# Retention and attention query/key projections as seven block products instead of eight, in a two-layer decoder trunk on one Trainium2 core

## The chip, the cores and the metric

The kernel runs on one core of a Trainium2 chip. The core has a matrix engine (PE, TensorE, whose weight loads are listed apart as PEld), a vector engine (DVE), a scalar engine (ACT), a general engine (POOL, GpSimd), a queue engine (SP) that mostly issues DMAs, and 16 DMA engines behind the queues. Matrix results land in PSUM, which this kernel uses as eight banks of 128 x 512 float32. The metric is the device time of one execution in microseconds, the median over runs; lower is better.

## The reference, cut to what matters

Two layers, each of a mixing sublayer and a SwiGLU feed-forward sublayer, on 512 tokens of width 1024, all in float32. The mixing sublayer starts from one wide projection of x, whose columns hold the queries, keys and values of the attention (three head groups of six heads of 64), the queries and keys (four heads of 256) and values and gates (four heads of 512) of the retention, and two merge gates.

```
z = einsum('bsd,dc->bsc', x, w_in) + b_in
q_a, k_a, v_a, q_r, k_r, v_r, g_r, gate_a, gate_b = split(z)
for group in 3 groups:                     # windows (128,1), (512,4), (2048,16)
    s = q k^T * 64**-0.5 + bias(relative position), masked to the window
    o, lse = softmax(s) v, log of the denominator
y_a = sum over groups of softmax(lse) * o

def rot(t):                                # halves t1, t2 of a retention head
    return concat(t1 * cos - t2 * sin, t1 * sin + t2 * cos)
q_r, k_r = rot(q_r), rot(k_r) / 16
y_r = retention(q_r, k_r, v_r)             # scores times a decay, then group norm
merged = sigmoid(gate_a) * (y_a @ w_attn_proj) + sigmoid(gate_b) * (silu(g_r) * y_r) @ w_ret_proj
x = layer_norm(ALPHA * x + merged @ w_out)
x = layer_norm(ALPHA * x + (silu(x @ w_gate) * (x @ w_up)) @ w_down)
```

## The kernel before

**Float32 from three products.** TensorE multiplies operands split in a high part (`act.copy`, a cast) and a low part (`dve.tensor_tensor`, the difference); `hilo` makes both. `mm3` then issues three matmuls: high by high, high by low, low by high. Every weight unit (`raw`, 128 x 1024 = 512 KB, loaded on SP's queue) is turned by `unit` or `Right.high` into `whi` (ACT) and `wlo` (DVE). The input is held transposed as `xh`/`xl`.

**Plain projections.** `pair_units` loads two units that hold 256 columns (two tiles of 128) of the weight over all eight blocks of the depth. `wstat(us, q)` multiplies one tile of 128 columns with all 512 tokens into one PSUM bank: 8 blocks x 3 matmuls of 512 columns. `wstat_halves` does the same in halves of 256 tokens at the kernel's start, for the first head pair, groups 0 and 1.

**Block products.** Most other projections go through `Right`: the product is cut in 2 x 2 blocks and computed with seven block products instead of eight. `ORDER` lists them; `S1` to `S4` are sums of quarters of x (in `xs`, made once per sublayer by `x_sums`), `P1` to `P4` are sums of quarters of the weight. P1 and P3 come from a second load that POOL issues with an addition (`accum_op`), P2 and P4 from an addition on DVE. `wide` runs it with the weights stationary and 256 tokens moving, so each matmul has 256 columns; `CHAIN` keeps three PSUM banks A, X and C, into which several products add up. `Right.operands` prepares the weights of the next product (load, cast on ACT; the low part on DVE is issued when its turn comes) while the current one runs. Before the change `wide` is used in the feed-forward sublayer and the merge gates, `tall` (tokens stationary) in values and gates.

**What runs beside the products.** `side` is a list of small pieces of work. Every step of a product calls `tick`, which takes the next pieces off that list at a rate set by `pace(us)`; `drain` issues all that is left at once. So the order of the instructions on each engine is fixed by hand, by the counts of steps. In the attention, `scores` (matmuls, a minimum on DVE at L536, an exponential on ACT at L538), `turn` (transposes L546, copy L547) and `values` of head pair `hp` are such pieces, and they run beside the projections `qk_units`/`wstat` of head pair `hp + 1`; each of them keeps two PSUM banks from its scores to its values. Two DMA round trips (`exd`, `mb`, `fa`, L574 to L593) that combine the head groups are issued from ACT. In the retention, the scores and outputs of head `h - 1` run beside the rotary, values and gates of head `h`.

**What the change touches.** `rotary(h)`: per query and key two `wstat`; the evacuation multiplies by cosine and sine with the bias added (L668), combines (L672, L673) and splits with `hilo` into a slot named `rot`, a slot per half of the head. `qk_units`, `qk_put` (a `tensor_scalar` on DVE that adds the bias and scales) and the loop over head pairs. `load`, `Right.load`, `bias_cols`, the order of the first loads in `layer`, and `ret_scores`, which reads the `rot` slots.

Of the kernel before, what the change touches and what calls it, by code (L numbers as in the profile page):

```python
# [53 lines left out]
def hybrid_kernel(ctx, tc, x, rel_bias, w_in, b_in, w_attn_proj, w_ret_proj, w_out,  # L54
# [44 lines left out]
    def work(name):  # L99
        return wk.tile([P, S], F32, tag="w2", name=name)  # L100
# [205 lines left out]
    class Right:  # L306
# [7 lines left out]
        def load(self, *names):  # L314
            for n in names:
                if (n, 0) in self.t:
                    continue
                for u, (a, b) in enumerate(self.shapes):
                    r = self.t[n, u] = load(self.src({"P1": "B11", "P3": "B12"}.get(n, n), u), a, b)
                    if n in ("P1", "P3"):  # L320
                        pool.dma_start(r, self.src({"P1": "B12", "P3": "B22"}[n], u), accum_op=ALU.add)  # L321

        def high(self, n):

# [298 lines left out]

    VB = 288

    bTs, braws = [], []
    for ly in range(DEPTH):
        bTs.append(sm.tile([P, COLS // P], F32, tag="bT", name="bT", bufs=2))
        braws.append(work("braw")[:COLS // P, :P])

    def bias_cols(ly):
        n = COLS // P
        px = psum()
        pe.transpose(px[:, :n], braws[ly], ident[:n, :n])
        dve.tensor_copy(bTs[ly], px[:, :n])

    def layer(ly, cp):
        w_l = rows(w_in[ly])
# [15 lines left out]
        def slot(name="op", dt=F32R):  # L654
            return opp.tile([P, 2, S], dt, tag="op", name=name)

        def rotary(h):

            rot = []
            for c0 in (C_QR + h * RQ, C_KR + h * RQ):  # L660
                us = pair_units(w_l, c0)
                prod = []
                for t in range(2):
                    ps = wstat(us, t)
                    pr = []
                    for tb in (cos, sin):
                        m = work("rp")
                        dve.scalar_tensor_tensor(out=m, in0=ps, scalar=bcol(c0 + t * P), in1=tb, op0=ALU.add, op1=ALU.mult)  # L668
                        pr.append(m)
                    prod.append(pr)  # L670
                (t1c, t1s), (t2c, t2s) = prod
                dve.tensor_tensor(out=t1c, in0=t1c, in1=t2s, op=ALU.subtract)  # L672
                dve.tensor_tensor(out=t1s, in0=t1s, in1=t2c, op=ALU.add)  # L673
                pair = []
                for src in (t1c, t1s):
                    o_ = slot("rot")
                    hilo(src, o_[:, 0], o_[:, 1])
                    pair.append(o_)
                rot.append(pair)
            heads[h]["q"], heads[h]["k"] = rot  # L680

        def ret_values_gates(h):
            cv, cg = C_VR + h * RV, C_GR + h * RV
# [18 lines left out]
        with stage("attn") as ap_, stage("attw", 4) as aw:  # L702
# [9 lines left out]
            def qk_put(hp, g, j, ps):  # L712
# [4 lines left out]
                    i_ = i_.rearrange("p (l r) -> p r l", r=4)  # L717
                dve.tensor_scalar(o_, i_, bcol(cc), (HD ** -0.5, 1.0)[j], op0=ALU.add, op1=ALU.mult)

            if ly == 0:  # L720
                x0 = [slot("x0", F32) for _ in range(NI)]
                warm = work("warm")
# [17 lines left out]
                load_x(2)  # L740
# [6 lines left out]
                for f in late:  # L747
                    f()
                us0 = [first, qk_units(0, 1)]
                load_x(3)  # L750
                side.extend([lambda l_=l_: bias_cols(l_) for l_ in range(DEPTH)] + vecs[:3] + ops[2] + vecs[3:] + ops[3])
                dve.tensor_tensor(out=pick, in0=ident[:, :NR], in1=ident[:, BK:BK + NR], op=ALU.add)
                rate[0], credit[0] = 0.4, 0.0
            else:
                us0 = [qk_units(0, g) for g in range(2)]
            for g in range(NG):
                qk_slot(0, g)
            pool.dma_start(cos, c_cos)
            pool.dma_start(sin, c_sin)
# [75 lines left out]
        with stage("ret") as rp:  # L835
            def ret_scores(h):
# [5 lines left out]
                def one(j):  # L842
                    n = S - j * P
                    ps = psum()[:, :n]
                    for d in range(2):
                        k_, q_ = heads[h]["k"][d], heads[h]["q"][d]
                        mm3(ps, k_[:, 0, j * P:(j + 1) * P], k_[:, 1, j * P:(j + 1) * P],
                            q_[:, 0, j * P:], q_[:, 1, j * P:], d == 0, d == 1)
                    t = work("pt")
                    dve.tensor_tensor(out=t[:, :n], in0=ps, in1=dec[:, :n], op=ALU.mult)  # L850
                    sl = heads[h]["p"][j]
# [354 lines left out]
```

## Time and profile before

| | us |
|---|---|
| median of three runs | 2185.17 (2185.1 to 2186.9) |
| the profiled execution | 2185.52 |
| its span in the trace | 2183.7 |
| mean granted TensorE clock | 0.997 |

The profiled execution's time lies 1.8 us above its span, which begins with the first and ends with the last instruction of the trace, and 0.35 us above the median. In the rows, a line such as `149.84 0.40 PE L82 MATMUL ps<-xh,whi` gives the start from the span's beginning, the duration, the engine, the line of the kernel, the operation and its output and inputs; what stands in brackets is the idle time before it and what ended that. Matmuls overlap their neighbours, so the distance between two starts is what one costs, not its duration. The stages of layer 0 in the trace: start to 20 us, first projections and attention values to 100, attention head pairs beside projections 100 to 206, the last pair beside rotary 0 and head 0's values and gates to 294, retention heads 1, 2 and 3 from 294 to 514 in three stretches of 73 us, then output and feed-forward; layer 1 repeats them from 1080 us.

### The profile page before, as it was taken

Reading aid. Unit: us, or ns where it says so; the run is one execution under the profiler, and the core shown is the slowest. Engines: PE = TensorE matmul, PEld = TensorE weight load, DVE = VectorE, ACT = ScalarE, POOL = GpSimd, SP = SyncE. Lnnn points to the kernel's source line nnn. Section 1 sums busy time; section 2 is a strip of 40 time slices with the busy share of each in tenths; the row PEclk is TensorE's granted clock in tenths of the full one; section 3 lists DMA queues with packets and bytes.
Section 4 is the critical chain, followed back from the end, with each engine's and each line's share of the span. In section 5 each row is a group of like instructions: output and inputs, shape, how many; then the busy total and the mean of one; then the engine's idle time right before and its main releaser. Section 6 shows DMA issues by size and latency. Waiting matters only on the chain.

```text
span 2183.7 us, 32442 instructions
## 1 busy us (share of the span) xinstructions
PE 2161.5 (99%) x12906; PEld 1902.4 (87%) x12906; DVE 1396.0 (64%) x2011; ACT 980.6 (45%) x1585; POOL 228.3 (10%) x253
## 2 busy tenths in 40 slices
PE   8999999999999999999999999999999999999998
PEld 7977788889988899989898778888899889999996
DVE  5643677777755685747675346767877447766575
ACT  4444544546633263525245445444556233544350
POOL 4100011011000100010020000111010001000001
PEclk9999999999999999999999999999999999999999
DMA  8944266458685356656269343565577762666551
GB/s 230 235 134 104 59 164 164 135 131 194 190 305 192 88 154 132 171 133 158 93 163 255 89 92 92 140 178 148 137 188 227 260 193 58 175 151 161 125 161 39
DMA packets 304954, 338.60 MB, mean 155 GB/s; under 512 B 21790, under 2 KB 243138, under 8 KB 304673
## 3 DMA queue, kind: packets, MB, share of 16 engines
q1 hardware_dynamic: 227712, 248.81, 37.8%
q0 software_dynamic: 49808, 74.90, 18.1%
q10 hardware_dynamic: 27280, 12.80, 2.1%
q8 instruction: 101, 1.65, 0.3%
q14 instruction: 53, 0.43, 0.1%
HBM read 310.67 MB, written 28.53 MB: 155 GB/s over the span
## 4 chain that ended last, share of the span: by engine, by line
PE 90%; issue 4%; DMA 3%; DVE 2%; POOL 1%; ACT 0%; SPq 0%; POOLq 0%; DVEq 0%; ACTq 0%
PE ps L82 81%; PE px L82 7%; DMA raw<-in_w_in 2%; PE px L546 1%; DMA exd<-wb 1%; PE px L878 1%; POOL ry L125 0%; DMA mb<-exd 0%; DMA exd<-pk 0%; PE px L170 0%; DVE xtok L1001 0%; DVE wlo L336 0%; ACT whi L330 0%; PE px L602 0%; DVE xtok L1010 0%
## 5 line engine op out<-in xcount | busy, mean ns | idle before, releaser
L336 DVE TENSOR_TENSOR wlo<-raw,whi 128x1024 fp32r<-128x1024 f32 (+1 forms) x364 | 417.9, 1150 | 214.1 <-ACT whi L330 212.9
L82 PE MATMUL ps<-xh,whi 128*128 128x256 f32 (+1 forms) x1536 | 516.6, 338 | 4.5 <-ACT whi L93 3.5
L330 ACT CAST whi<-raw 128x1024 fp32r<-128x1024 f32 (+1 forms) x364 | 359.0, 990 | 345.4 <-PE ps L82 205.3
L82 PE MATMUL ps<-xh,wlo 128*128 128x256 f32 (+1 forms) x1536 | 500.9, 327 | 1.0 <-DVE wlo L94 1.0
L82 PE MATMUL ps<-xl,whi 128*128 128x256 f32 (+1 forms) x1536 | 501.2, 327 | 0.2 <-DVE xl L94 0.2
L82 PE MATMUL ps<-xs,whi 128*128 128x256 f32 (+1 forms) x2048 | 404.6, 296 | 0.0
L82 PEld LDWEIGHTS ps<-xs,whi 128*128 128x128 f32 x2048 | 327.7, 191 | 10.3
L94 DVE TENSOR_TENSOR wlo<-raw,whi 128x1024 fp32r<-128x1024 f32 (+2 forms) x162 | 193.3, 1196 | 202.0 <-ACT whi L93 201.0
L82 PEld LDWEIGHTS ps<-xh,whi 128*128 128x128 f32 x1536 | 292.4, 191 | 34.3 <-issue 5.7
L82 PEld LDWEIGHTS ps<-xh,wlo 128*128 128x128 f32 x1536 | 292.9, 191 | 26.5 <-DVE wlo L94 1.2
L82 PEld LDWEIGHTS ps<-xl,whi 128*128 128x128 f32 x1536 | 293.7, 191 | 19.5 <-DVE xl L94 1.0
L82 PE MATMUL ps<-xs,wlo 128*128 128x256 f32 (+1 forms) x1024 | 303.4, 296 | 0.0
L93 ACT CAST whi<-raw 128x1024 fp32r<-128x1024 f32 (+2 forms) x162 | 166.0, 1027 | 240.8 <-PE ps L82 150.7
L82 PE MATMUL ps<-whi,xs 128*128 128x512 f32 (+1 forms) x768 | 219.6, 360 | 0.6 <-ACT whi L330 0.4
L82 PEld LDWEIGHTS ps<-xs,wlo 128*128 128x128 f32 x1024 | 196.0, 191 | 5.0
L82 PE MATMUL ps<-whi,ht 128*128 128x512 f32 x576 | 178.4, 389 | 0.0
L82 PEld LDWEIGHTS ps<-whi,xs 128*128 128x128 f32 x768 | 137.7, 188 | 21.1 <-ACT sn L466 1.0
L82 PE MATMUL ps<-wlo,xs 128*128 128x512 f32 (+1 forms) x384 | 138.1, 360 | 0.8 <-DVE wlo L336 0.8
L321 POOL DMA_DIRECT2D raw<-in_w_in x64 | 79.2, 1263 | 472.9 <-DMA raw<-in_w_in 159.8
L82 PEld LDWEIGHTS ps<-whi,ht 128*128 128x128 f32 x576 | 108.2, 188 | 22.3
L321 POOL DMA_DIRECT2D raw<-in_w_ffn_gate x40 | 51.8, 1295 | 679.4 <-DMA raw<-in_w_ffn_up 251.4
L347 DVE TENSOR_TENSOR raw<-raw 128x1024 f32<-128x1024 f32 (+1 forms) x104 | 119.5, 1149 | 2.7 <-DMA raw<-in_w_in 0.5
(183 smaller groups left out, 2897.0 us busy)
## 6 DMA issues: line engine op xcount, KB each, us to landing
raw<-in_w_in SPq DMA_DIRECT2D x152, 512.0 KB, 4.3
raw<-in_w_ffn_up SPq DMA_DIRECT2D x64, 512.0 KB, 4.1
raw<-in_w_in POOLq DMA_DIRECT2D x48, 512.0 KB, 6.9
raw<-in_w_ffn_gate SPq DMA_DIRECT2D x44, 512.0 KB, 4.6
raw<-in_w_ffn_down SPq DMA_DIRECT2D x44, 512.0 KB, 4.2
raw<-in_w_ffn_gate POOLq DMA_DIRECT2D x40, 512.0 KB, 6.7
raw<-in_w_in SPq DMA_DIRECT2D x72, 256.0 KB, 4.9
raw<-in_w_ret_proj SPq DMA_DIRECT2D x32, 512.0 KB, 6.1
```

Of the source, the lines that this page charges most:

```text
L82: pe.matmul(ps, lhsT=a, rhs=b, start=start, stop=stop, skip_group_check=True)
L93: act.copy(out=hi, in_=src)
L94: dve.tensor_tensor(out=lo, in0=src, in1=hi.bitcast(F32), op=ALU.subtract)
L321: pool.dma_start(r, self.src({"P1": "B12", "P3": "B22"}[n], u), accum_op=ALU.add)
L330: act.copy(out=h, in_=src)
L336: dve.tensor_tensor(out=l, in0=src, in1=h.bitcast(F32), op=ALU.subtract)
L347: dve.tensor_tensor(out=r, in0=r, in1=self.t["B22" if n == "P2" else "B21", u], op=ALU.add)
L546: pe.transpose(px[:, (2 + j) * P:(3 + j) * P], s[:, hh, j * P:(j + 1) * P], ident)
L878: pe.transpose(px[:, t * P:(t + 1) * P], ys[i][:, t * P:(t + 1) * P], ident)
```

## The change

1. `rotary(h)` for heads 1 to 3 computes queries and keys of a head in one `wide` call of seven products (query columns as the left, key columns as the right half of the weight). Head 0 keeps `wstat`. The evacuation works on quarters (two tiles by 256 tokens): the bias is added by ACT (`biased_copy`), quarters are combined on DVE, and `turned` rotates each. The `rot` slots now hold both halves of the head in high and in low part; `ret_scores` reads them so.
2. In the attention's head pairs 1 and 2, groups 0 and 1 go through one `wide` call (`qk_group`): queries of the two groups as the left, keys as the right half. ACT writes the results with bias and scale (`put`; scaled biases of the queries in the new `bQs`). Group 2 keeps `wstat`. A load whose columns lie in two places is issued in two pieces (`pieces`).
3. In layer 0 the cosine and sine tables are loaded on SP's queue behind the four loads of x instead of on POOL's; the third load of x stands later in the program's text.

```diff
     def load(src, a, b):
         v = view(raw(), a, b)
-        nc.sync.dma_start(v, src)
+        for v_, s_ in pieces(v, src):
+            nc.sync.dma_start(v_, s_)
         return v
...
+        act.mul(out=bQs[ly], in_=px[:, C_QA // P:C_QA // P + NQ], mul=HD ** -0.5)
...
+        def turned(t, ts_, hi, lo):
+            n = t.shape[2]
+            s = view(work("rs"), 2, n)
+            cs, sn_ = (a[:, ts_].unsqueeze(1).to_broadcast([P, 2, n]) for a in (cos, sin))
+            dve.tensor_tensor(out=s, in0=t, in1=sn_, op=ALU.mult)
+            dve.tensor_tensor(out=t, in0=t, in1=cs, op=ALU.mult)
+            dve.tensor_tensor(out=t[:, 0], in0=t[:, 0], in1=s[:, 1], op=ALU.subtract)
+            dve.tensor_tensor(out=t[:, 1], in0=t[:, 1], in1=s[:, 0], op=ALU.add)
+            hilo(t, hi[:, :, ts_], lo[:, :, ts_])
         def rotary(h):
...
+            def biased_copy(ps, c, sign=1.0):
+                o_ = view(work("sn"), 2, 256)
+                for q in range(2):
+                    act.activation(out=o_[:, q], in_=ps[:, q * 256:(q + 1) * 256], func=AF.Identity, bias=bcol(c + q * P), scale=sign)
+                return o_
+            def ev(i, ps):
+                p2 = ps.rearrange("p (q t) -> p q t", q=2)
+                if i in (1, 5):
+                    sn[i] = biased_copy(ps, cq if i == 1 else ck)
+                elif i == 6:
+                    sn[i] = biased_copy(ps, ck, -1.0)
+                elif i == 2:
+                    dve.tensor_tensor(out=sn[1], in0=p2, in1=sn[1], op=ALU.add)
+                    turned(sn[1], slice(0, 256), *heads[h]["q"])
+                elif i == 7:
+                    dve.tensor_tensor(out=sn[5], in0=sn[5], in1=p2, op=ALU.subtract)
+                    turned(sn[5], slice(256, 512), *heads[h]["k"])
+                elif i == 3:
+                    dve.tensor_tensor(out=sn[6], in0=p2, in1=sn[6], op=ALU.add)
+                    turned(sn[6], slice(0, 256), *heads[h]["k"])
+                elif i == 4:
+                    turned(biased_copy(ps, cq), slice(256, 512), *heads[h]["q"])
+            wide(pair_right(w_l[:, :, cq:], w_l[:, :, ck:], 0), x_left, ev)
...
+            def qk_group(hp):
...
+                def put(v, j, half):
+                    for g in range(2):
...
+                        act.activation(out=o_, in_=i_, func=AF.Identity, bias=bs[:, c:c + 1], scale=(HD ** -0.5, 1.0)[j])
...
+                wide(Right(src, [(4, 256)], WIDE, ("B11", "P1", "B22", "P3", "B21")), x_left, ev)
...
                 if hp:
                     for g in range(NG):
+                        qk_slot(hp, g)
+                    qk_group(hp)
+                    for g in range(2, NG):
                         us = qk_units(hp, g)
-                        qk_slot(hp, g)
```

Three places in the order of the instructions. The first is the vector engine at the end of the rotary of head 1 in layer 0. `wlo` is the low part of a weight unit, `rp` were the products with cosine and sine, `sn` is now a quarter with its bias and `rs` its product with sine, `rot` the split result. Before:

```order
L336 TENSOR_TENSOR wlo<-raw,whi 128x1024
L668 SCALAR_TENSOR_TENSOR rp<-ps,bT,cos 128x512
L668 SCALAR_TENSOR_TENSOR rp<-ps,bT,sin 128x512
L673 TENSOR_TENSOR rp<-rp 128x512
L672 TENSOR_TENSOR rp<-rp 128x512
L336 TENSOR_TENSOR wlo<-raw,whi 128x1024
L94 TENSOR_TENSOR rot<-rp,rot 128x512 x2
L336 TENSOR_TENSOR wlo<-raw,whi 128x1024
```

After, at the same place:

```order
L724 TENSOR_TENSOR sn<-ps,sn 128x512
L94 TENSOR_TENSOR rot<-sn,rot 128x2x256
L676 TENSOR_TENSOR sn<-sn,rs 128x256
L677 TENSOR_TENSOR sn<-sn,rs 128x256
L674 TENSOR_TENSOR rs<-sn,sin 128x512
L345 TENSOR_TENSOR wlo<-raw,whi 128x1024
L94 TENSOR_TENSOR rot<-sn,rot 128x2x256
L675 TENSOR_TENSOR sn<-sn,cos 128x512
L674 TENSOR_TENSOR rs<-sn,sin 128x512
L676 TENSOR_TENSOR sn<-sn,rs 128x256
L677 TENSOR_TENSOR sn<-sn,rs 128x256
```

The tail of the rotation now runs among the first operations of the following values (`L724`, and the low parts of their weights at `L345`).

The second place is TensorE in layer 0, head pair 2's projections with the scores of head pair 1 beside them. `px<-qk` are scores, `px<-v,sT` value products, `px<-ident,s` the transposes of the softmax. Before:

```order
L82 MATMUL px<-qk 128x256 x2
L82 MATMUL ps<-xh,whi 128x512
L82 MATMUL ps<-xl,whi 128x512
L82 MATMUL ps<-xh,wlo 128x512
L82 MATMUL px<-v,sT 128x64 x2
L82 MATMUL ps<-xh,whi 128x512
L82 MATMUL ps<-xl,whi 128x512
L82 MATMUL ps<-xh,wlo 128x512
L546 MATMUL px<-ident,s 128x128 x4
```

After:

```order
L82 MATMUL px<-qk 128x256 x2
L82 MATMUL ps<-xs,whi 128x256 x2
L82 MATMUL ps<-xs,wlo 128x256
L82 MATMUL px<-v,sT 128x64 x2
L555 MATMUL px<-ident,s 128x128 x8
L82 MATMUL ps<-xs,whi 128x256 x3
L82 MATMUL ps<-xh,whi 128x256
L82 MATMUL ps<-xl,whi 128x256
```

Two groups of four transposes now stand together, right behind the value products, where one group stood behind three more long matmuls.

The third place is the scalar engine around the second round trip of the same stage. Before:

```order
L589 DMA exd_1176<-wb 128x4x2
L557 COPY y<-px 128x64 x2
L593 DMA fa<-exd_1176 128x8
L93 CAST whi<-raw 128x1024
L538 ACTIVATE s,ls<-s,nm 128x128 x2
L538 ACTIVATE s,ls<-s,nm 128x256 x2
L547 COPY sT<-px 128x128 x2
```

After:

```order
L598 DMA exd_1180<-wb 128x4x2
L339 CAST whi<-raw 128x1024
L794 COPY sn<-ps 128x512
L547 ACTIVATE s,ls<-s,nm 128x128 x2
L602 DMA fa<-exd_1180 128x8
L339 CAST whi<-raw 128x1024
L794 COPY sn<-ps 128x512
L547 ACTIVATE s,ls<-s,nm 128x256 x2
L556 COPY sT<-px 128x128 x2
```

A cast, a copy of a product and an exponential now stand between the two transfers, where two small copies stood.

More of the change, by code (lines that the diff above doesn't have):

```diff
@@ L109, in load, with pieces @@
         v = view(raw(), a, b)
-        nc.sync.dma_start(v, src)
-        return v
+        for v_, s_ in pieces(v, src):
+            nc.sync.dma_start(v_, s_)
+        return v
+    def pieces(v, src):
+        if len(src.shape) == 3:
+            return [(v, src)]
+        n = src.shape[3]
+        return [(v[:, :, g * n:(g + 1) * n], src[:, :, g]) for g in range(src.shape[2])]
     def unit(v):
@@ L655, in slot @@
             return opp.tile([P, 2, S], dt, tag="op", name=name)
-        def rotary(h):
[L659 to L680, printed above, removed]
+        def turned(t, ts_, hi, lo):
[7 more added lines that the diff above has]
+            hilo(t, hi[:, :, ts_], lo[:, :, ts_])
@@ L739, in layer @@
                 first, make = qk_units(0, 0, pair_apart)
-                load_x(2)
                 cp = x_copies()
@@ L749, in layer @@
                 us0 = [first, qk_units(0, 1)]
+                load_x(2)
                 load_x(3)
+                nc.sync.dma_start(cos, c_cos)
+                nc.sync.dma_start(sin, c_sin)
                 side.extend([lambda l_=l_: bias_cols(l_) for l_ in range(DEPTH)] + vecs[:3] + ops[2] + vecs[3:] + ops[3])
```

68 lines of the change are left out of this document (61 added, 7 removed).

## Prediction

> **What bounds the kernel now.** I read the engine totals first, then the chain of work that ended last, then the waits of TensorE, and only then single stretches of the timeline.
>
> ```profile
> PE 2161.5 (99%) x12906; PEld 1902.4 (87%) x12906; DVE 1396.0 (64%) x2011; ACT 980.6 (45%) x1585; POOL 228.3 (10%) x253
> PE 90%; issue 4%; DMA 3%; DVE 2%; POOL 1%; ACT 0%; SPq 0%; POOLq 0%; DVEq 0%; ACTq 0%
> PE ps L82 <- ACT whi L93: 3.5, 2, 2.1
> ...
> PE ps L82 <- ACT sn L466: 0.2, 1, 0.2
> ```
>
> TensorE is busy for 99% of the span and is 90% of the chain. The last two rows are the first and the last of ten in the list of TensorE's waits (total us, times, longest); the ten add up to 12.9 us of 2183.7. So time is won by giving TensorE less to do, and lost where another engine comes to stand in front of it.
>
> **The tensor work of one conversion.** The change converts ten products: one per rotary of heads 1 to 3 and one per head pair 1 and 2 of the attention, in both layers. A conversion drops 96 matmuls of 512 columns (4 tiles, 8 blocks of the depth, 3 each) and issues 168 of 256 columns (7 products, 2 halves, 4 blocks, 3 each). Matmuls are pipelined, so the price is the distance of starts: first and last of 18 matmuls of the old form, and of the 24 of one block product in the feed-forward part.
>
> ```profile
> 149.84 0.40 PE L82 MATMUL ps<-xh,whi 128*128 128x512 f32 x1
> ...
> 153.71 0.39 PE L82 MATMUL ps<-xh,wlo 128*128 128x512 f32 x1
> 801.43 0.28 PE L82 MATMUL ps<-xh,whi 128*128 128x256 f32 x1
> ...
> 804.19 0.28 PE L82 MATMUL ps<-xh,wlo 128*128 128x256 f32 x1
> ```
>
> 3.87 us over 17 steps is 0.2276 us; 2.76 over 23 is 0.120. Old: 96 x 0.2276 = 21.85 us. New: 168 x 0.120 = 20.16. Each conversion saves 1.69 us, ten save **16.9 us**. Break-even would be a short matmul at 21.85/168 = 0.130 us, so 0.010 us of each is all the gain there is.
>
> The Trainium skill (TensorE: Matmul & The Clock Gate, "Back-to-back issue gap") states sustained spacings of about 81 ns at 128 columns and 131 ns at 512, from which I estimate 98 ns at 256, three quarters of the long one instead of half. By that ratio the change would lose; both rows above speak against it, since 0.120 is 53% of 0.2276.
>
> **The rotary: VectorE.** Rows of the same stage of head 1 give VectorE's distances, back to back.
>
> ```profile
> 304.33 0.75 DVE L668 SCALAR_TENSOR_TENSOR rp<-ps,bT,cos 128x512 f32<-128x512 f32 x1
> 304.99 0.74 DVE L668 SCALAR_TENSOR_TENSOR rp<-ps,bT,sin 128x512 f32<-128x512 f32 x1
> 305.65 0.68 DVE L673 TENSOR_TENSOR rp<-rp 128x512 f32<-128x512 f32 x1
> 306.25 0.68 DVE L672 TENSOR_TENSOR rp<-rp 128x512 f32<-128x512 f32 x1
> 306.85 1.22 DVE L336 TENSOR_TENSOR wlo<-raw,whi 128x1024 fp32r<-128x1024 f32 x1
> 307.99 0.69 DVE L868 BATCH_NORM_STATS2 st<-px 128x6 f32<-128x512 f32 x1
> ...
> 284.25 0.42 DVE L850 TENSOR_TENSOR pt<-px,dec 128x256 f32<-128x256 f32 x1
> 284.58 1.21 DVE L94 TENSOR_TENSOR wlo<-raw,whi 128x1024 fp32r<-128x1024 f32 x1
> ```
>
> A fused multiply of 512 columns is 0.66 us, a plain operation of 512 0.60, of 256 0.33, a low part of a weight unit (1024) 1.14. Removed per rotary: 8 x 0.66 + 4 x 0.60 + 4 low parts x 0.60 = 10.1 us. Added: 3 more low parts x 1.14, 2 sums of raw weights (P2, P4) x 1.14, 3 additions x 0.60, and four calls of `turned`, each 3 x 0.60 + 2 x 0.33 = 2.46: 17.3 us. Net +7.3 us. The next view has, per stretch, its length and then the busy time of PE, PEld, DVE, ACT and POOL, the clock, the DMA share and GB/s; the first is rotary, values and gates of head 1, the second its rotary alone.
>
> ```profile
> 294.00:367.50 73.50, 73.50 (x339) 61.08 (x338) 54.78 (x87) 35.62 (x49) 7.73 (x9) 1.00 0.58 151
> 294.64:322.00 27.36, 27.36 (x129) 22.59 (x129) 19.42 (x42) 10.45 (x15) 4.14 (x5) 1.00 0.71 172
> ```
>
> VectorE gets 19.4 + 7.3 = 26.7 us of work in a rotary of 27.4 - 1.7 = 25.7 us: it is full, but over the whole stage it has 62 of 71.8 us, so the backlog is passed on to the values. What TensorE needs from it inside the rotary are the low parts of the next weights, and in the new order these stand ahead of most of `turned`. Following that order by hand with these distances, the last low parts are ready 0.1 to 0.7 us before their matmuls, the last one with nothing to spare. Lower bound 0 (all in time); upper bound 1.2 us per rotary (one `turned`'s half in front of a low part). I take 0.3, near the lower end since the hand trace found no late one: 6 x 0.3 = **+1.8 us**, range 0 to 7. Bias copies move to ScalarE, which is busy 10.5 of 27.4 us there; the two accumulating loads per conversion go to POOL, 4.1 of 27.4 us busy, and the fifth 512 KB load to SP's queue at a DMA share of 0.71. I price these at nothing: they are covered as long as TensorE's 25.7 us last, and a weight that came late would be a wait on `whi`, of about one cast.
>
> **ScalarE's queue in the attention.** ScalarE holds the DMA round trips that combine the groups; between issuing the second one's two halves it stands still.
>
> ```profile
> 147.15 0.37 ACTq L589 DMA_DIRECT2D exd<-wb  x1
> ...
> 152.08 1.05 ACT L93 CAST whi<-raw 128x1024 fp32r<-128x1024 f32 x1 [3.28 <-DMA exd<-wb]
> ```
>
> A cast of 1024 columns is 1.05 us. In the new order the cast that waited moves ahead of the second half. Unless other queued work hides it, that is a few tenths of gain or loss; I set it at nothing, inside the range of the next part.
>
> **Between scores and transposes.** In the attention the copies with bias go from VectorE to ScalarE: three more casts (3.15 us), eight copies of 256 columns and three plain ones, each at about the 0.50 of the exponential below or less: some 8 us more.
>
> ```profile
> 100.00:152.00 52.00, 52.00 (x296) 41.31 (x296) 21.27 (x56) 23.44 (x75) 3.31 (x6) 1.00 0.61 171
> L538 ACT ACTIVATE s<-s,nm 128x256 f32<-128x256 f32 x84 | 42.1, 502 | 63.4 <-DVE nm L536 61.1 <-issue 2.3
> L536 DVE CUSTOM_DVE_ANT_0 s<-px,bias 128x256 f32<-128x256 f32 x84 | 32.4, 421 | 55.4 <-PE px L82 55.4
> 160.53 0.70 PE L82 MATMUL px<-qk 64*128 64x256 f32 x4
> 161.16 0.50 PE L82 MATMUL ps<-xh,whi 128*128 128x512 f32 x1
> ...
> 161.96 0.55 PE L82 MATMUL px<-v,sT 128*128 128x64 f32 x4
> 162.32 0.48 PE L82 MATMUL ps<-xh,whi 128*128 128x512 f32 x1
> ...
> 163.10 0.60 PE L546 MATMUL px<-ident,s 128*128 128x128 f32 x4
> 163.46 0.48 PE L82 MATMUL ps<-xh,whi 128*128 128x512 f32 x1
> ```
>
> As a share it is harmless (23.4 + 8 of 50 us). What counts is the chain scores, VectorE's minimum (0.42 each of two), ScalarE's exponential (0.50), transposes. Before, the transposes start 2.57 us after their scores and do not wait. After the change a product holds three banks of PSUM, not one or two, and three blocks of scores want six of the eight. The new order of TensorE shows what that does in head pair 2: after two scores come three short matmuls, two value products and then eight transposes in a row. Cover from the rows: 2 scores 0.32, 3 x 0.120 = 0.36, 2 values 0.18, 4 transposes 0.36, in all 1.22 us. The chain needs at least 0.3 + 2 x 0.42 + 0.50 = 1.64 and was 2.57 with no wait, so TensorE waits 0.4 to 1.35 us, and up to 2.4 if a cast of 1.05 stands ahead of the exponential. I take 1.65, toward the upper end as ScalarE has more in its queue: +3.3 us for two layers. At the end of each converted head pair the remaining turn and values are drained under six long matmuls (1.37 us) where nine stood (2.05): 0.6 of that 0.68 on the path, four times, +2.4. Together **+5.7 us**. Range: 0 if all is covered, 14.4 if four events reach 2.0 us and then run as the next rows show.
>
> ```profile
> 207.14 0.39 PE L82 MATMUL ps<-xh,wlo 128*128 128x512 f32 x1
> 209.14 0.71 PE L546 MATMUL px<-ident,s 128*128 128x128 f32 x2 [1.61 <-ACT s L538]
> ...
> 1277.24 0.40 PE L82 MATMUL ps<-xh,wlo 128*128 128x512 f32 x1
> 1279.63 0.55 PE L82 MATMUL px<-v,sT 128*128 128x64 f32 x3 [2.00 <-ACT sT L547]
> 1280.55 0.68 PE L82 MATMUL ps<-xh,whi 128*128 128x512 f32 x1
> ...
> 1284.02 0.42 PE L82 MATMUL ps<-xh,wlo 128*128 128x512 f32 x1
> 1281.00:1283.00 2.00, 2.00 (x6) 1.58 (x5) 1.28 (x2) 1.27 (x3) 0.00 (x0) 0.50 0.13 2
> ```
>
> A wait of 1.61 us cost itself. After the wait of 2.00 us the granted clock is 0.50, and eight matmuls take 3.47 us, 0.434 each instead of 0.228: another 1.65 us. So 2.0 us of waiting costs 3.7. The Trainium skill (same page, Part 1) has the half clock come after an idle window of about 3.4 us; this trace shows it after 2.00, so here the page is too lenient.
>
> **The start.** The two 256 KB tables go behind the activations' loads.
>
> ```profile
> 8.00:10.00 2.00, 1.04 (x10) 0.80 (x8) 1.62 (x3) 2.00 (x5) 1.29 (x3) 1.00 1.18 309
> 13.14 0.39 PE L82 MATMUL ps<-xh,whi 128*128 128x256 f32 x1 [2.14 <-ACT whi L93]
> 20.14 1.05 ACT L93 CAST whi<-raw 128x1024 fp32r<-128x1024 f32 x1 [0.77 <-DMA raw<-in_w_in]
> ```
>
> At 309 GB/s 0.52 MB is 1.7 us, which could come off the 2.14 us wait for the first weights. But the second unit, cast at 20.14, still has the same bytes ahead of it and TensorE needs it then. I take **-0.5 us** (range -2 to +1.5).
>
> **Sum.** -16.9 + 1.8 + 5.7 - 0.5 = -9.9 us. The profiled execution took 2185.52 us (span 2183.7, the rest lies around it), which gives 2175.6; the median of the runs is 0.35 us lower: **2175.3 us**. A difference below 0.2%, 4.4 us, can hardly be told from no change.
>
> **Rivals.** (1) VectorE bounds the rotaries: the backlog grows and each low part there comes late by a `turned`, 1.0 to 2.0 us per rotary instead of 0.3, or +4 to +10: -5.7 to 0.3, 2179.5 to 2185.5. For it: 26.7 us of work in 25.7. Against: what TensorE needs stands first. (2) Slower: ScalarE's queue makes TensorE wait 2.0 us twice per converted head pair, each followed by the half clock. Place: transposes and value products in the attention. Price: 8 x 3.7 = 29.6, sum -16.9 + 1.8 - 0.5 + 29.6 = +14, 2199 us. It decides (slower by 4.4) once an event costs 2.5 us (15.6 + 4.4 = 20.0 over 8). For it: 1279.63. Against: most transposes still have a product's worth of cover. By the idle window of the Trainium skill cited above no half clock would follow, and it would be 8 x 2.0 = 16, a net of about 0. (3) No wait at all, 16.9 + 0.5 off: 2168 us. (4) Short matmuls do not keep 0.120 us beside rotary work: at three quarters of 0.2276, 0.171, a conversion costs 28.7 and ten cost +68, 2253 us; the feed-forward row above speaks against it. The spacing rule of the Trainium skill cited above is this rival's. (5) The saving and the waits cancel over many small ones: no change.
>
> **Chances.** Forecast 0.55, (1) 0.17, (2) 0.10, (3) 0.12, (4) 0.01, (5) 0.05. Faster by over 0.2%: the forecast, (3) and half of (1), 0.75; within 0.2%: the rest of (1) and (5), 0.14; slower: (2) and (4), 0.11. The range runs from full gain to the upper end of (1): 2167.5 to 2186.5.
>
> **What would show it.** In the profile after: block products of 256 columns at 0.120 us distance in the rotary and attention stretches (else rival 4); rotary stretches near 25.7 us and no wait on `wlo` over 0.5 us (else rival 1); a wait of 1 to 2 us at the eight transposes in head pair 2; granted clock 1.00 throughout the attention (else rival 2); a first-weight wait below 2.14 us. What would make the forecast wrong is above all the price of waits in the attention, which no row of before measures.

## The result: slower by 1.6%

The changed kernel takes 2219.77 us (median of five runs, 2215.35 to 2229.04) against 2185.33 (five runs of the kernel before): a ratio of 1.0162, 95% interval 1.0140 to 1.0185, or 34.4 us lost where 9.9 were forecast as won. The profiled execution has a span of 2218.0 us, 34.3 more than before. These are its totals, its chain of work that ended last, and the list of TensorE's waits (total us, times, longest; first three and last of ten rows).

```profile
PE 2162.5 (97%) x13626; PEld 1939.5 (87%) x13626; DVE 1454.6 (66%) x2099; ACT 1051.3 (47%) x1709; POOL 263.4 (12%) x279
PE 82%; DMA 6%; DVE 5%; issue 5%; ACT 1%; POOL 1%; POOLq 0%; DVEq 0%; ACTq 0%; SPq 0%
PE ps L82 <- DVE wlo L345: 16.2, 12, 3.6
PE px L555 <- ACT s L547: 9.3, 3, 5.5
PE ps L82 <- ACT whi L339: 9.1, 2, 4.9
...
PE ps L82 <- DVE xl L94: 0.2, 1, 0.2
```

TensorE's waits have grown from 12.9 to 46.4 us, by 33.5. Its busy time has hardly moved (2161.5 to 2162.5), although a kernel with these same 13626 matmuls and few of the waits, shown at the end, is busy for 2144.6, which is 16.9 less than before and 17.9 less than the changed kernel. So -16.9 + 17.9 + 33.5 = 34.5. Most of the 17.9 is a lower granted clock: by the clock records of the traces 31.5 us of the changed kernel's matmuls ran at half clock and 3.4 us of the other's, which I estimate at half of the difference, 14 us. What the remaining 4 us are was not traced.

The short matmuls themselves are as forecast, here the first block product of the attention's head pair 1, 24 starts in 2.75 us, 0.120 us each:

```profile
101.28 0.28 PE L82 MATMUL ps<-xh,whi 128*128 128x256 f32 x1
...
104.03 0.28 PE L82 MATMUL ps<-xh,wlo 128*128 128x256 f32 x1
```

By the two sustained spacings of the Trainium skill (TensorE: Matmul & The Clock Gate, "Back-to-back issue gap"), 81 ns at 128 columns and 131 ns at 512, I would estimate them at three quarters of a long one; the trace has 53%.

The long waits sit in three places. **Place 1, start of head pair 1's projections.** Rows of the timeline (start, duration, engine, what was idle before and what ended that):

```profile
96.89 2.61 POOL L330 DMA_DIRECT2D raw<-in_w_in  x2 [17.38 <-DVE wlo L345]
108.15 1.04 ACT L339 CAST whi<-raw 128x1024 fp32r<-128x1024 f32 x1 [9.63 <-DMA raw<-in_w_in]
109.25 0.80 PE L82 MATMUL ps<-xs,whi 128*128 128x256 f32 x2 [4.94 <-ACT whi L339]
106.00:108.00 2.00, 0.00 (x0) 0.00 (x0) 0.00 (x0) 0.00 (x0) 1.03 (x1) 0.64 1.30 210
109.00:117.00 8.00, 7.29 (x32) 6.55 (x33) 6.57 (x10) 4.67 (x9) 0.00 (x0) 0.51 1.08 278
```

P1's first load is issued in two pieces at 91.3 and 92.0 and lands at 96.3 and 97.2. Only then does its second, accumulating load go out, in two pieces from 96.9, and lands at 108.1 among transfers that keep the DMA engines full (a share of 1.30 in the window 106 to 108). Its cast stands at the head of ScalarE's queue for 9.6 us; TensorE, done with B11 at 104, waits 4.94 and then runs at 0.51 of the clock for eight us. Layer 1 has the same with 4.15 us at 1208.

**Place 2, the stage after head pair 2.**

```profile
212.01 0.38 ACTq L598 DMA_DIRECT2D exd<-wb  x1
217.43 0.34 ACTq L602 DMA_DIRECT2D fa<-exd  x1
223.35 0.69 DVE L606 TENSOR_TENSOR y<-y,fa 128x512 f32<-128x512 f32 x1 [9.18 <-DMA fa<-exd]
223.96 0.42 DVE L545 CUSTOM_DVE_ANT_0 s<-px,bias 128x256 f32<-128x256 f32 x1
224.42 0.51 ACT L547 ACTIVATE s<-s,nm 128x256 f32<-128x256 f32 x1 [6.18 <-DVE nm L545]
225.07 1.18 PE L555 MATMUL px<-ident,s 128*128 128x128 f32 x4 [5.53 <-ACT s L547]
```

The list names ScalarE, which waits for VectorE, which waits for the group factors `fa` on their way through memory. The scaling at L606 stands in VectorE's queue ahead of the scores' minimum, and so in front of transposes that have nothing to do with it. Before, the same two transfers took 4.9 and 2.6 us (issued at 200.12 and 205.00, the second landed at 207.57); now 5.4 and 5.8. The queue is not new. Before, the same scaling and the same minimum stood one behind the other, and the wait of 1.61 us that the prediction shows at 209.14 is the end of this chain:

```profile
207.67 0.68 DVE L597 TENSOR_TENSOR y<-y,fa 128x512 f32<-128x512 f32 x1
208.27 0.28 DVE L536 CUSTOM_DVE_ANT_0 s<-px,bias 128x128 f32<-128x128 f32 x1
```

The change has made it 3.9 us longer in layer 0.

**Place 3, the first weights of the values behind each block-product rotary.**

```profile
327.86 1.20 POOL L330 DMA_DIRECT2D raw<-in_w_in  x1 [8.97 <-DMA raw<-in_w_in]
328.62 1.05 POOL L133 TENSOR_TENSOR ry<-ve,mhalf 128x1 f32<-128x1 f32 x1
329.70 0.22 DVE L134 SCALAR_TENSOR_TENSOR rt<-ry,ve 128x1 f32<-128x1 f32 x1 [4.32 <-POOL ry L133]
...
410.92 0.69 DVE L674 TENSOR_TENSOR rs<-sn,sin 128x512 f32<-128x512 f32 x1 [3.27 <-DMA y_d<-yt]
411.53 1.22 DVE L345 TENSOR_TENSOR wlo<-raw,whi 128x1024 fp32r<-128x1024 f32 x1
412.80 0.50 PE L82 MATMUL ps<-wlo,xh 128*128 128x512 f32 x1 [3.61 <-DVE wlo L345]
```

VectorE is not out of time here; it stands still. Once for a power of one column on GpSimd, queued behind an accumulating load that waits for its first load; once for a buffer: `rs` is taken from the ring of six (`work`) that also holds `yt`, and `yt` is held until its store has landed. The low part that TensorE wants is next in the queue.

### The profile page after: what moved, and what is told of

Read it like the earlier page. It is cut to its first block, busy times and chain, and to the rows that moved or that the text cites. A ratio compares the mean times of both kernels' runs of the same rounds, so it can differ in the third digit from the quotient of the medians.

```text
span 2218.0 us, 34254 instructions
## 1 busy us (share of the span) xinstructions
PE 2162.5 (97%) x13626; PEld 1939.5 (87%) x13626; DVE 1454.6 (66%) x2099; ACT 1051.3 (47%) x1709; POOL 263.4 (12%) x279
## 3 DMA queue, kind: packets, MB, share of 16 engines
q8 instruction: 106, 1.74, 0.3%
## 4 chain that ended last, share of the span: by engine, by line
PE 82%; DMA 6%; DVE 5%; issue 5%; ACT 1%; POOL 1%; POOLq 0%; DVEq 0%; ACTq 0%; SPq 0%
PE ps L82 74%; PE px L82 6%; DMA raw<-in_w_in 3%; DVE wlo L345 2%; DMA y_d<-yt 1%; DMA exd<-wb 1%; PE px L555 1%; DMA fa<-exd 1%; ACT whi L339 1%; POOL ry L133 1%; DVE rs L674 0%; DVE sn L675 0%; PE px L178 0%; POOL raw L330 0%; DVE xtok L1094 0%
## 5 line engine op out<-in xcount | busy, mean ns | idle before, releaser
L345 DVE TENSOR_TENSOR wlo<-raw,whi 128x1024 fp32r<-128x1024 f32 (+1 forms) x434 | 502.9, 1162 | 263.6 <-ACT whi L339 252.4
L339 ACT CAST whi<-raw 128x1024 fp32r<-128x1024 f32 (+1 forms) x434 | 432.9, 1000 | 427.6 <-PE ps L82 228.3
L82 PE MATMUL ps<-xs,whi 128*128 128x256 f32 (+1 forms) x2688 | 532.7, 297 | 9.1 <-ACT whi L339 9.1
L82 PE MATMUL ps<-xh,whi 128*128 128x256 f32 (+1 forms) x1456 | 453.5, 313 | 5.3 <-ACT whi L93 4.2
L82 PEld LDWEIGHTS ps<-xs,whi 128*128 128x128 f32 x2688 | 431.5, 193 | 24.2 <-ACT whi L339 9.5
L82 PE MATMUL ps<-xh,wlo 128*128 128x256 f32 (+1 forms) x1456 | 443.1, 305 | 1.0 <-DVE wlo L94 1.0
L82 PE MATMUL ps<-xl,whi 128*128 128x256 f32 (+1 forms) x1456 | 443.7, 306 | 0.2 <-DVE xl L94 0.2
L82 PE MATMUL ps<-xs,wlo 128*128 128x256 f32 (+1 forms) x1344 | 396.2, 295 | 1.2 <-DVE wlo L345 1.2
L82 PEld LDWEIGHTS ps<-xs,wlo 128*128 128x128 f32 x1344 | 259.2, 193 | 6.9 <-DVE wlo L345 1.7
L94 DVE TENSOR_TENSOR wlo<-raw,whi 128x1024 fp32r<-128x1024 f32 (+2 forms) x122 | 144.5, 1187 | 177.5 <-ACT whi L93 177.1
```

Source lines behind the costliest of these rows:

```text
L82: pe.matmul(ps, lhsT=a, rhs=b, start=start, stop=stop, skip_group_check=True)
L94: dve.tensor_tensor(out=lo, in0=src, in1=hi.bitcast(F32), op=ALU.subtract)
L339: act.copy(out=h, in_=src)
L345: dve.tensor_tensor(out=l, in0=src, in1=h.bitcast(F32), op=ALU.subtract)
```

## The experiments

Ratios are to the kernel before on the same chip, whose median was 2185.78 in the first four, 2187.51 in the next four and 2184.45 in the last four. The changed kernel was not run again beside them, so a difference from its 2219.77 carries the few us by which these sessions differ.

The traces tell in which stage a gain lies. In the table, "attention" runs from the last matmul of the attention's values (128x288) to the first score product of retention head 0, "retention" from there to the first score product of head 3; both layers are added, in us of the one profiled execution. With the saved work alone (4 and 6 conversions of 1.69 us) they would be 341.4 and 421.3.

| kernel | attention | retention |
|---|---|---|
| before | 348.1 | 431.4 |
| changed | 370.6 | 443.7 |
| rotaries alone | 346.9 | 443.1 |
| attention alone | 371.4 | 431.3 |
| `rs` in its own buffer | 375.6 | 425.6 |
| power left out | 372.5 | 421.0 |
| group 2 first | 370.3 | 435.3 |
| sums on VectorE | 356.2 | 438.1 |
| scaling on GpSimd | 364.1 | 437.1 |
| repairs, accumulating loads | 352.1 | 422.6 |
| repairs, sums on VectorE, groups first | 343.9 | 421.6 |
| repairs, sums on VectorE, group 2 first | 339.5 | 422.7 |

The three kernels whose edit lies in the attention alone (group 2 first, sums, scaling) are 6 to 8 us shorter than the changed kernel in the retention, which they do not touch. Whether that is the spread of executions (2215.35 to 2229.04 for the changed kernel) or something passed on from stage to stage is open; it is no gain of the edited place.

**Each half alone.** The attention's projections put back (and the first loads), and, in the other kernel, the rotaries:

```diff
-                        qk_slot(hp, g)
-                    qk_group(hp)
-                    for g in range(2, NG):
+                    for g in range(NG):
                         us = qk_units(hp, g)
+                        qk_slot(hp, g)
```
```diff
-            if h == 0:
+            if True:
                 for c0, n_ in ((cq, "q"), (ck, "k")):
```

> The rotaries of heads 1 to 3 as block products; attention projections and the first loads as before. The changed kernel loses 34.4 us against before. Theory P (three places that lose by themselves): in the changed trace the time from the first score product of head 0 to that of head 3 has grown by 8.1 us in layer 0 and 4.9 in layer 1, so this kernel alone loses about 13 us: 2198. Rival Q (the retention only inherits late transfers from the attention): the waits there go and the tensor work saved shows, 6 x 1.7: 2175.

> Queries and keys of two attention groups as block products for head pairs 1 and 2; rotaries and first loads as before. Theory P: the rest of the loss less about 1 us for the start, +20 us: 2205, with TensorE waiting 4 to 5 us on the weights of the second block product at the start of head pair 1 in both layers, half clock behind it, and 3 to 6 us in front of transposes in the stage after head pair 2. Rival Q: all of the loss, +34 or more.

Rotaries alone: 2194.71 us, 1.0046 (1.0031 to 1.0061). Attention alone: 2209.49, 1.0111 (1.0096 to 1.0126). The losses, 8.9 and 23.7, add up to 32.6 of 34.4: the halves lose each by itself, and rival Q falls. The losses lie where theory P put them, 3.3 us smaller and 4.5 us larger than it named (2198 and 2205). The attention alone waits 5.04 and 5.03 us for the second block product's weights. The rotaries' first wait rows:

```profile
PE ps L82 <- DVE wlo L345: 11.3, 11, 2.1
PE px L966 <- ACT yb L961: 5.3, 3, 2.8
```

**Place 3: the ring and the power.**

```diff
-            s = view(work("rs"), 2, n)
+            s = view(box["rp"].tile([P, S], F32, tag="rs", name="rs", bufs=1), 2, n)
```
```diff
-        pool.tensor_tensor(out=y, in0=ve, in1=mhalf, op=ALU.pow)
+        dve.tensor_scalar(y, ve, 0.0, 1e-3, op0=ALU.mult, op1=ALU.add) if quick else pool.tensor_tensor(out=y, in0=ve, in1=mhalf, op=ALU.pow)
...
-                    rs = rstd_of(mv[:, 1:2])
+                    rs = rstd_of(mv[:, 1:2], True)
```

> The changed kernel, but the products with sine in the rotation (rs) have a buffer of their own instead of one of the ring of six that they share with the transposed outputs, which stay there until their store has landed. Theory B (buffer): VectorE's idle times of 3.3, 1.8 and 2.5 us before rs, ended by that store, go; TensorE's waits on low parts at the start of the values of heads 2 and 3 shrink by as much, with the half clock behind the two of over 3 us: about -11 us, 2209. Rival V (VectorE has simply too much to do in these stages): its work is the same, so the waits stay: within 3 us of the changed kernel, 2217 to 2222.

> The changed kernel with the inverse square root of the retention's group norm left out of GpSimd: a constant from VectorE stands in its place, so the normalisation is not that of the reference; VectorE has one small operation more per block. Theory G (GpSimd's queue): VectorE's idle times of 4.3, 1.4, 2.8, 2.1 and 1.6 us behind the power, which stands in GpSimd's queue behind accumulating loads that wait for their first load, go; the waits on low parts at the start of the values shrink by 1.5 us in most of six places: -6 to -12 us, 2207 to 2214. Rival V: no more than 2 us.

With `rs` in its own buffer 2204.84 us, 1.0085 (1.0069 to 1.0102); with the power left out 2202.59, 1.0081 (1.0056 to 1.0105): 15 and 17 us less than the changed kernel, and 18 and 23 in the retention by the table; theories B and G had 11 and 6 to 12. The wait on `wlo`, 16.2 us in the changed kernel, is now, in the kernel with the buffer and in the one without the power:

```profile
PE ps L82 <- DVE wlo L345: 0.9, 2, 0.5
PE ps L82 <- DVE wlo L345: 1.2, 3, 0.5
```

VectorE's work is practically the same (1453.2 and 1455.6 us against 1454.6), so rival V, a VectorE with too much to do, falls. That either edit is enough suggests one chain: a late power makes `yb` late, so its transposes and their store, so the ring's buffer, so `rs`, so the low part behind it. For it: without the power no idle time over 1 us before `rs` is left. But its first links are argued, not shown. The store that ended the 3.27 us at 410.92 was issued 8.6 us after the one before it, with the power and without; it was on its way for 10.1 us with the power and 5.2 without, and why was not traced.

In the kernel with the buffer VectorE still waits for the power, but the low part no longer stands far behind it. The first two rows are from this kernel, the third from the changed one, where VectorE takes up the power's result at 329.70:

```profile
332.79 0.22 DVE L134 SCALAR_TENSOR_TENSOR rt<-ry,ve 128x1 f32<-128x1 f32 x1 [3.59 <-POOL ry L133]
333.59 1.22 DVE L345 TENSOR_TENSOR wlo<-raw,whi 128x1024 fp32r<-128x1024 f32 x1
334.91 1.22 DVE L345 TENSOR_TENSOR wlo<-raw,whi 128x1024 fp32r<-128x1024 f32 x1
```

So the new buffer also changes the order: the low part comes 0.8 us behind the power instead of 5.2, and at this place, where nothing waited for the ring, the order alone is enough to take TensorE's wait of 1.64 us away. How much of the 15 us is order and how much the waiting for the ring was not separated. TensorE still notices the power elsewhere: its waits on `yb` grow from 1.3 to 3.8 us.

**Place 1: lead time, or the accumulating load?** Group 2 first:

```diff
-                    qk_group(hp)
                     for g in range(2, NG):
                         us = qk_units(hp, g)
                         for j in range(2):
                             qk_put(hp, g, j, wstat(us, j))
+                    qk_group(hp)
```

> The changed kernel with the order of the projections inside head pairs 1 and 2 turned round: group 2's plain products first, then the block products of groups 0 and 1. Theory L (lead time): the second block product's weights are a load and then an accumulating load, and at the start of head pair 1 they have one block product, 2.9 us, as cover; 10.9 us of plain products in front of them remove TensorE's waits of 5.4 and 4.9 us there and most of the half clock behind them (about 4 and 2 us): -16 us, 2204. Rival T (throughput): the DMA engines are full at that place, so the wait only moves to a later product or to the end of the stage: less than 5 us gained, 2215 or more.

2212.26 us, 1.0114 (1.0099 to 1.0129): about 7 us less, between the two. But by the table the attention has gained nothing (370.3 against 370.6); the 7 us lie in the retention, so at this place rival T holds and lead time for TensorE alone is not enough. (Its expectation and the next one name waits of 5.4 and 4.9 us; in the changed kernel they are 4.94 and 4.15.) TensorE no longer waits for the weight, but at the same place for something else:

```profile
114.81 0.86 PE L555 MATMUL px<-ident,s 128*128 128x128 f32 x2 [5.54 <-ACT s L547]
```

Then the accumulating loads taken out: VectorE adds blocks that are loaded once.

```diff
+            elif n in ("P1", "P3") and ("B12", 0) in self.t:
+                r, o = self.t["B11" if n == "P1" else "B12", 0], self.t["B12" if n == "P1" else "B22", 0]
+                dve.tensor_tensor(out=r, in0=r, in1=o, op=ALU.add)
+                self.t[n, 0] = r
...
-                wide(Right(src, [(4, 256)], WIDE, ("B11", "P1", "B22", "P3", "B21")), x_left, ev)
+                wide(Right(src, [(4, 256)], WIDE, ("B11", "B12", "B22", "B21")), x_left, ev)
```

> The changed kernel, but in the attention's block products the sums of weight blocks P1 and P3 are made by VectorE from blocks that are loaded once, instead of by a second, accumulating load of 512 KB each on GpSimd's queue (four loads instead of five plus two; two more VectorE operations of 1.14 us per conversion). Theory A (the late accumulating load is what TensorE waits for at the start of head pair 1, whether its weights are wanted by TensorE first or stand at the head of ScalarE's queue): the waits of 5.4 and 4.9 us and the half clock behind them go: -12 to -16 us, 2204 to 2208. Rival M (ScalarE's and VectorE's queues or PSUM make the wait): no more than 4 us.

2201.15 us, 1.0082 (1.0062 to 1.0102): 19 us less, 14.4 of it in the attention, as theory A had it. No wait on `whi L339` is left in its list. The edit takes away the dependent step and three loads of 512 KB per conversion at once; which of the two counts was not separated. And the wait of place 2 in layer 0 has shrunk without being touched, from 5.53 us to 2.08:

```profile
211.74 0.93 PE L559 MATMUL px<-ident,s 128*128 128x128 f32 x4 [2.08 <-ACT s L551]
```

This fits that the round trip shares the DMA engines with these loads; the share itself was not varied apart.

**Place 2: who stands behind the round trip?**

```diff
-            dve.tensor_tensor(out=yv, in0=yv, in1=fa[:, od]...
+            (pool if od else dve).tensor_tensor(out=yv, in0=yv, in1=fa[:, od]...
```

> The changed kernel with one operation moved from VectorE to GpSimd: the scaling of the second pair of attention groups (y times fa), which waits for the factors' round trip through memory. Theory F (VectorE's queue stands behind that round trip, and the scores' minimum behind it): TensorE's waits in front of transposes and value products after head pair 2 (5.5 us in layer 0, 2.7 in layer 1, and some of the 1.8, 1.1 and 0.7 around them) go, with the half clock behind the long ones (about 3 us each): -10 to -14 us, 2206 to 2210. Rival S (ScalarE itself is late, or GpSimd's accumulating loads now stand behind the round trip and come late): no gain, 2217 to 2222.

2207.0 us, 1.0095 (1.0079 to 1.0110): 13 us less, inside theory F's range, but only 6.5 of them lie in the attention. Theory F has the cause, since no wait for `s` is left in the list, and rival S falls; it had the gain twice too large, and that the sum fits is luck. One wait of 2.8 us on the turned scores is left, and GpSimd's scaling makes TensorE wait 1.1 us once:

```profile
PE px L82 <- ACT sT L556: 5.3, 4, 2.8
PE px L611 <- POOL y L606: 1.1, 1, 1.1
```

**Only the rotaries, repaired.** The first kernel above with `rs` in its own buffer.

> Only the rotaries of heads 1 to 3 as block products (attention and first loads as before), with rs in a buffer of its own. Theory B: the 11.3 us of waits on low parts that the rotaries alone still had go, and with them what separates 2194.7 from the full saving of 6 x 1.7 us: 2176 to 2180, clearly faster than before. Rival V (VectorE is at its limit, 26.7 us of work in 25.7): no better than before, 2185 or more.

2181.47 us, 0.9976 (0.9965 to 0.9987): faster than before by 5 to 6 us, half of the 10.1 of saved work and short of the 2176 to 2180 that theory B named. What remains is in its list: 4.9 us for `yb`, which is the late power (VectorE waits 4.31 and 4.92 us for it just before the two), and 3.5 for the scores, of which before had 1.6.

```profile
PE px L966 <- ACT yb L961: 4.9, 2, 2.5
PE px L555 <- ACT s L547: 3.5, 2, 1.9
```

**The repairs together.** First with group 2 in front and accumulating loads.

> The changed kernel with all repairs together: rs in its own buffer, group 2 first, the scaling on GpSimd, the first loads as before. If the three places lose independently, the gains add up (-15, -16, -12, -1): 2174 to 2178; with every wait gone it would be 16.9 us under before, 2168. If the attention's block products lose by something else than these two waits (banks of PSUM, ScalarE's queue), it stays above 2185.

2180.39 us, 0.9978 (0.9963 to 0.9993), less than the sum of gains, since the delay of place 1 is only displaced:

```profile
109.99 1.04 ACT L339 CAST whi<-raw 128x1024 fp32r<-128x1024 f32 x1 [9.51 <-DMA raw<-in_w_in]
111.06 1.23 DVE L345 TENSOR_TENSOR wlo<-raw,whi 128x1024 fp32r<-128x1024 f32 x1 [9.63 <-ACT whi L339]
113.46 0.28 DVE L545 CUSTOM_DVE_ANT_0 s<-px,bias 128x128 f32<-128x128 f32 x1
114.34 0.86 PE L555 MATMUL px<-ident,s 128*128 128x128 f32 x2 [4.71 <-ACT s L547]
```

The cast of the late weight, wanted by TensorE only later now, stands at the head of ScalarE's and VectorE's queues, and the scores' minimum and exponential behind it. With the sums on VectorE, in both orders:

> The repairs together, with the sums of the attention on VectorE and the order of the groups as in the changed kernel: rs in its own buffer, scaling on GpSimd, first loads as before. Theory: the two waits left in the repaired kernel (4.7 and 5.0 us, with half clock behind them about 4 us each) go: 2180.4 - 18 gives 2162 as a limit; full saving of tensor work without any new wait is 2185.3 - 16.9 = 2168.4: 2166 to 2171. Rival: the waits come back in another place as they did when group 2 was put first: 2176 or more.

> As the last one, with group 2's plain products first in each head pair. If the sums on VectorE have removed the cause, the order of the groups no longer matters: within 3 us of it. If lead time still counts, this one is faster by more than 3 us.

Groups first: 2175.07 us, 0.9956 (0.9942 to 0.9970), between theory and rival, its profiled execution the fastest of five at 2168.11. Group 2 first: 2166.69, 0.9919 (0.9907 to 0.9932), the fastest version of all, 17.8 us under before. The order still mattered, by 8 us and not 3. That it does so by lead time is the expectation's reading and not shown: what the other executions of the former waited for was not seen, as only the fastest was traced, and that one lies 1.4 us from the traced one of the latter. Group 2 first in the profile:

```profile
PE 2144.6 (99%) x13626; PEld 1928.4 (89%) x13626; DVE 1463.8 (68%) x2101; ACT 1047.0 (48%) x1709; POOL 251.7 (12%) x271
PE ps L82 <- ACT whi L93: 3.3, 2, 1.9
PE px L615 <- POOL y L610: 2.2, 2, 1.1
...
PE ps L82 <- DVE xl L94: 0.2, 1, 0.2
```

TensorE is busy 16.9 us less than before, and its waits add up to 11.0 us in eight rows, 1.9 less than before. Its attention, 339.5 us in the table, is no longer than the saved work alone would make it, so the three banks of PSUM that a product now holds cost nothing that shows.

**The first loads alone**, in the kernel before.

> The kernel before with the order of the first loads alone changed. In the changed trace the first transposes of the third block of x start 1.1 us later than before: 2186.4. Rival: the prediction's term, -0.5 us: 2184.8. Both may be too small to tell from no change.

2185.66 us, 1.0006 (0.9997 to 1.0015): no difference that can be told. The first weights come earlier (TensorE starts on them at 11.97 us instead of 13.14), and the second unit's are then what is waited for:

```profile
20.74 0.46 PE L82 MATMUL ps<-xh,whi 128*128 128x256 f32 x1 [2.89 <-ACT whi L93]
```

## Why the prediction was wrong, step by step

**The tensor work, -16.9: right.** 2161.5 - 2144.6 = 16.9 in a kernel where little hides it. That it fits to the tenth is luck: the kernel before ran 6.8 us of its matmuls at half clock and this one 3.4, an estimate of 1.7 us, so the saved work itself is nearer 15.

**The rotary, +1.8 (0 to 7): wrong.** Alone the rotaries lost 8.9 us against 10.1 saved, so this term was 19. The step that failed is the hand trace of VectorE's order "with these distances": it lets VectorE run without a pause, and it ends with the rotary. In time there they were: all of TensorE's waits on low parts in the retention stand at the first weights of the values, where "the backlog is passed on to the values" had no price. VectorE's amount of work, which the prediction weighed, was not the trouble; two of its operations wait for others, and the low parts stand behind them. The rows of before had the one (VectorE waited up to 7.46 us for the same power on GpSimd, harmlessly then), and the ring of six was not looked at, though the change takes `sn` and `rs` from it.

**The attention, +5.7 (0 to 14.4): wrong by the largest sum.** Alone it lost 23.7 against 6.8 saved, a term of 30. The wait that the prediction worked out, at the eight transposes of head pair 2, is there in size: 1.83 us in layer 0, at the value products just ahead of them, and 1.05 in layer 1, 2.9 where 3.3 stood. That is in part luck, since in layer 0 the scores' minimum stood behind a low part whose cast on ScalarE had stood 3.63 us behind the round trip. What failed are two sentences that priced things at nothing. "The two accumulating loads per conversion go to POOL" counted GpSimd's busy time and not when the second load can start and land; at head pair 1 that was 5.8 us from the issue of the first load to its landing and then 11.2 us for the second, against 2.9 us of cover. And the round trip's "few tenths of gain or loss" was waits of 5.53 and 2.71 us where 1.61 and none had stood: the prediction looked at what stands between the two halves on ScalarE, not at what stands behind the factors on VectorE, and read the 1.61 us only as the price of a wait. (The upper end of 14.4 is its four events at 3.6 us; at the 3.65 us of its own rows they are 14.6.)

**The half clock** was priced rightly for its shortest stretch (1.65 us lost; the stretches of 3.41 us cost 1.7) and given too few and too short events: the changed kernel has seven stretches at half clock before its end, of 3.41 to 10.24 us, and loses, by the estimate above, about 14 us more than the repaired one. Rival 2, at 0.10, had the sign and the half clock. Its price for the attention, 29.6, against the measured 30 is luck: it counted eight waits of 2.0 us, where there were few and longer ones. It named ScalarE's queue behind the scores, where the late weight and the round trip were the cause.

**The start, -0.5 (-2 to 1.5):** 1.2 us the other way, inside its range, and not to be told from nothing.

**Rival 1** had the place (low parts that come late on VectorE) and only part of the mechanism: the low part at 334.91 does stand behind a `turned`, but a VectorE that is full is not the cause, as the same work with `rs` in its own buffer brought 15 us back.

## What to carry to other kernels

An operation that is "off the path" by its busy time can still be what everything waits for, if it stands in an in-order queue behind a transfer: list for each added operation what it waits for, and what is queued behind it, buffer releases included. A load in two dependent steps needs the time of both as cover; here, where the DMA engines were full, adding two blocks on an engine with room was worth 14 us against accumulating in flight. A wait's new end is not yet a gain: compare the stages, since one total can mix the edited place with places that the edit does not touch. And a saving of 1% on the bounding engine is lost to waits of the same size: price these first.

## What the runs showed of the hardware

The granted clock does not follow the length of a wait alone. In the changed kernel it dropped behind waits of 2.48 us (at the start), 2.71 and more and did not behind 1.83 or 1.64; before, 2.00 was enough. But with the rotaries alone it stayed at 1.00 behind a wait of 2.76 us (up to 319.13), and with the scaling on GpSimd it fell to 0.50 behind one of 1.72 us (up to 170.24). The windows behind the waits of 2.71 and 1.59 us in the changed kernel, then these two:

```profile
1321.00:1326.00 5.00, 4.25 (x18) 2.72 (x18) 2.28 (x9) 2.14 (x9) 0.00 (x0) 0.66 0.16 29
488.00:490.00 2.00, 1.96 (x9) 1.62 (x10) 2.00 (x4) 0.01 (x1) 0.00 (x0) 1.00 0.44 34
316.00:327.00 11.00, 6.61 (x32) 5.07 (x31) 10.23 (x21) 6.80 (x12) 0.73 (x2) 1.00 0.63 141
170.70:174.10 3.40, 3.40 (x18) 3.40 (x18) 0.53 (x1) 3.38 (x12) 0.00 (x0) 0.50 0.23 84
```

The clock records of the traces show more. Within one trace all changes of the clock lie on one grid of 3.413 us: the drops of the changed kernel at 21.21, 106.54, 222.59 and 413.74 us are 25, 34 and 56 steps apart. What counts is how long TensorE stands still within one step. Past the first 25 us of the fourteen traces, each of the 33 steps at full clock with more than 1.74 us in which no matmul ran was followed by half clock, and none of those with less than 1.63, so about half a step decides. The wait of 2.76 us was split over two steps, 1.27 and 1.49 us.

The Trainium skill (TensorE: Matmul & The Clock Gate, Part 1) puts the threshold at an idle window of about 3.4 us; here about half of such a step was enough.
